# Attention: the prompt's scores, softmax and transpositions of a pair of heads queued ahead of the first half's units

## Chip, cores and metric

One core of a Trainium2 chip runs the whole program. The metric is the device time of one execution in microseconds (us). Three runs of the kernel before took 3154.69, 3155.14 and 3159.97 us; their median is 3155.14.

## What is computed

One inference step of a backbone with four layers. 512 latent tokens and 128 prompt (context) tokens of width 1024 run through them with the same weights. Each layer is a token mixer and a SwiGLU, both with adaLN modulation and a gated residual. The mixer of layer 0 is 2-D neighbourhood attention with a relative-position bias, of layer 1 banded sliding-window attention with a sink, of layer 2 multi-head latent attention, of layer 3 grouped-query attention; all have 16 heads. Cut to what matters for the change:

```python
def block_attention(q, k, v, sink=None):              # the prompt: its own keys only
    ...
    def one_block(qi):
        s = jnp.einsum('bqhgd,bkhd->bhgqk', qi, k).astype(jnp.float32) * scale
        (p,) = joint_softmax([s], sk)
        return jnp.einsum('bhgqk,bkhd->bqhgd', p.astype(v.dtype), v)

# in each layer
op = heads_out(block_attention(qp, kp_, vp_), na_w_o[r])                          # prompt
os_ = heads_out(na_latent_attention(qs, ks_, vs_, cache_na_k[:, r], ...), ...)    # latent tokens
xp = xp + mp[2] * op
xs = xs + ms[2] * os_
xp = xp + mp[5] * swiglu(...)
xs = xs + ms[5] * swiglu(...)
```

The 128 prompt tokens attend to themselves alone; the 512 latent tokens attend to a selection of latent keys and to 128 cached ones.

## The kernel before

Each fp32 product outside the scores is made of three matmuls of high and low parts (`whi`, `wlo`, `hh`, `hl`). A layer's attention runs in `Attn.units()` (line 955): 16 units u = 0 to 15, four groups g of four heads, two pairs of heads `pr` in each, two halves `hf` of the latent tokens (256 each) for every pair; u = 4g + 2pr + hf. `half_pair` (line 1140) is one unit. It calls `blocks`, which makes four blocks of 128 latent queries by one head: scores into a PSUM tile `S`, softmax (maximum on VectorE, exponentials on ScalarE, a reciprocal, scaling on GpSimd), transpositions of the probabilities through a PSUM tile `tp` (line 1055), and their copy to `pt` by ScalarE or VectorE in turn (lines 286 and 288). Then come the products with the values, `sm<-pt,v`, one run without gaps (`run_of`), and the output is put away.

Between the blocks `tick` (line 937) runs background jobs: the next group's projections, the preparation of its queries and keys, the output projection, the modulation of later stages. Their matmuls, mostly `sm<-whi,hh` and the like, fill TensorE while softmaxes run; they are called fillers below. Blocks are issued with a priority raised by `AHEAD` = 100. What stands in which place on each engine is set by the tile framework's scheduler, from the order of the program, the raised priorities and its own estimate of times; buffers of a tile are handed out in the order of the program. `S` has three buffers in layers 0 and 1 and two in layers 2 and 3, `tp` two, the prompt's `pp` and `ptp` one.

The prompt's part of a pair is `prompt` (line 1102), called through `prompt_group`. It takes one `S` tile, makes the 128 x 128 scores of two heads (4 matmuls, in layer 2 6), one maximum for both (`stp`, line 1116), two exponentials (`pp`, line 1122), a reciprocal (line 1128), two scalings (line 1130), two transpositions (`tp<-consts,pp`) and one copy (`ptp`). Its products with the values, `sm<-ptp,v`, stand in the run of the pair's second half, in both kernels.

In layer 0 a pair's keys are transposed (`tp<-consts,qs`), scaled into 64 partitions, and copied to the other 64 by a DMA from SP's queue, `k<-k` (`double`, line 1050). The same queue carries the biases (`bias<-in_nabias`, 576 KB each) and the modulation weights (`rawm<-in_wmod`, four of 512 KB in a burst).

Of the kernel before, what the change touches and what calls it, by code (L numbers as in the profile page):

```python
# [910 lines left out]
class Attn:  # L911
# [228 lines left out]
    def half_pair(self, g, pr, hf):  # L1140
        net = self.net
        u = 4 * g + 2 * pr + hf
        own = self.prompt_group(g, pr) if hf else None
        vals = self.blocks(g, pr, hf, u)
        with net.tc.high_priority(offset=AHEAD):
            o = net.ps()
            net.run_of(self.pv(o[:, :256], vals) + (self.pv(o[:, 256:384], own) if hf else []))
            self.put_o(self.o_tile(2 * g + pr), o[:, :256], hf)
            if hf:
                self.put(self.o_tile(2 * g + pr), slice(NL, T), o[:, 256:384])  # L1150
# [659 lines left out]
```

## Time and profile before

| | us |
|---|---|
| median of three runs | 3155.14 |
| profiled execution | 3159.6 |
| its span (first to last instruction) | 3157.8 |
| TensorE busy in it | 3021.5 (96%) |
| VectorE, ScalarE, GpSimd busy | 2112.1, 1518.0, 612.7 |
| four attention loops, first score to last product with values | 296, 204, 253, 203 |

The profile is of one execution. Times within it count from the start of the span. An engine's idle time ahead of an instruction is put down to whoever released the semaphore it waited for. The granted clock is TensorE's, as a share of full speed.

### The profile page before, as it was taken

How to read it: one execution, taken by the hardware profiler on the slowest of the kernel's cores; microseconds unless marked ns; L12 is line 12 of the kernel's file. 1: busy time of each engine (PE TensorE's matmuls, PEld its weight loads, DVE VectorE, ACT ScalarE, POOL GpSimd, SP SyncE). 2: the span in 40 equal slices, each digit the busy share in tenths (PEclk: the TensorE clock that was granted, in tenths of full speed). 3: DMA queues.
4: the chain of work that ended last, by engine and by line, in shares of the span. 5: the costliest groups of instructions: out<-in, count | busy, mean ns of one | idle time of the engine just before them, and what ended most of it. 6: DMA issues, size and time to landing. Idle time of an engine off the chain costs nothing. (4 is left out here: it accounts for less than half of the span.)

```text
span 3157.8 us, 57354 instructions
## 1 busy us (share of the span) xinstructions
PE 3021.5 (96%) x21997; PEld 2844.8 (90%) x21997; DVE 2112.1 (67%) x4442; ACT 1518.0 (48%) x3248; POOL 612.7 (19%) x691
## 2 busy tenths in 40 slices
PE   7998999999999999999988899999999999999999
PEld 6997889999988789999986678999998878999999
DVE  5555486666577768585767776857575765876765
ACT  4455453343346755242446675534243566543432
POOL 2453210000045430000025553000002553100000
PEclk9998999999999999999998999999999999999999
DMA  8347544232433333222214223432223211232322
GB/s 267 92 127 215 179 132 150 93 121 89 136 128 105 136 117 118 84 82 83 81 54 144 66 62 109 160 108 81 81 86 114 56 33 28 62 104 67 97 69 82
DMA packets 159025, 331.40 MB, mean 105 GB/s; under 512 B 18592, under 2 KB 40480, under 8 KB 158752
## 3 DMA queue, kind: packets, MB, share of 16 engines
q1 hardware_dynamic: 155584, 323.46, 33.0%
q10 hardware_dynamic: 3168, 4.28, 0.4%
q8 instruction: 173, 2.83, 0.4%
q14 instruction: 100, 0.82, 0.1%
HBM read 303.86 MB, written 4.28 MB: 98 GB/s over the span
## 5 line engine op out<-in xcount | busy, mean ns | idle before, releaser
L271 PE MATMUL big<-hl,whi 128*128 128x320 f32 x2688 | 814.9, 309 | 1.8 <-DVE hl L1045 1.8
L271 PE MATMUL big<-hh,whi 128*128 128x320 f32 x2688 | 811.1, 310 | 1.6 <-ACT whi L319 1.1
L271 PE MATMUL big<-hh,wlo 128*128 128x320 f32 x2688 | 808.5, 310 | 0.0
L319 ACT CAST whi<-raw 128x512 fp32r<-128x512 f32 (+2 forms) x644 | 387.4, 607 | 687.0 <-PE big L271 536.7
L320 POOL TENSOR_TENSOR wlo<-raw,whi 128x512 fp32r<-128x512 f32 (+2 forms) x148 | 206.9, 1413 | 1583.0 <-ACT whi L319 1550.4
L271 PEld LDWEIGHTS big<-hh,whi 128*128 128x128 f32 x2688 | 499.2, 188 | 10.3 <-issue 3.2
L271 PEld LDWEIGHTS big<-hl,whi 128*128 128x128 f32 x2688 | 501.4, 188 | 3.5 <-DVE hl L1045 2.8
L271 PEld LDWEIGHTS big<-hh,wlo 128*128 128x128 f32 x2688 | 499.4, 188 | 0.3
L320 DVE TENSOR_TENSOR wlo<-raw,whi 128x512 fp32r<-128x512 f32 (+1 forms) x496 | 330.6, 671 | 152.2 <-ACT whi L319 146.8
L319 ACT CAST whi<-sum 128x512 fp32r<-128x512 f32 x320 | 197.3, 620 | 278.6 <-PE big L271 240.7
L271 PE MATMUL big<-ah,wlo 128*128 128x320 f32 x1408 | 329.1, 309 | 0.0
L271 PE MATMUL big<-ah,whi 128*128 128x320 f32 x1408 | 329.0, 310 | 0.0
L271 PE MATMUL big<-al,whi 128*128 128x320 f32 x1408 | 328.5, 309 | 0.0
L1087 POOL TENSOR_SCALAR p<-p,st 128x640 f32<-128x640 f32 (+2 forms) x256 | 195.3, 768 | 300.2 <-DVE st L1086 177.3
L320 DVE TENSOR_TENSOR wlo<-sum,whi 128x512 fp32r<-128x512 f32 x320 | 218.5, 685 | 45.3 <-ACT whi L319 43.2
L609 DVE SCALAR_TENSOR_TENSOR x<-big,mod,x 128x128 f32<-128x128 f32 (+2 forms) x384 | 146.4, 433 | 152.7 <-PE big L271 151.7
L271 PEld LDWEIGHTS big<-ah,whi 128*128 128x128 f32 x1408 | 237.2, 188 | 1.3 <-issue 0.8
L271 PEld LDWEIGHTS big<-al,whi 128*128 128x128 f32 x1408 | 237.3, 188 | 0.3
L271 PEld LDWEIGHTS big<-ah,wlo 128*128 128x128 f32 x1408 | 237.3, 188 | 0.2
L271 PE MATMUL sm<-whi,hh 128*128 128x256 f32 (+1 forms) x770 | 224.9, 297 | 3.4 <-ACT qs L286 2.2
L271 PE MATMUL sm<-whi,hl 128*128 128x256 f32 (+1 forms) x770 | 223.6, 292 | 0.0
L271 PE MATMUL sm<-wlo,hh 128*128 128x256 f32 (+1 forms) x770 | 223.4, 292 | 0.1
(268 smaller groups left out, 5454.0 us busy)
## 6 DMA issues: line engine op xcount, KB each, us to landing
raw<-in_wall SPq DMA_DIRECT2D x676, 256.0 KB, 2.6
rawm<-in_wmod SPq DMA_DIRECT2D x176, 512.0 KB, 5.9
k<-k SPq DMA_DIRECT2D x38, 384.0 KB, 4.1
bias<-in_nabias SPq DMA_DIRECT2D x16, 576.0 KB, 7.2
raw<-in_wmod SPq DMA_DIRECT2D x32, 256.0 KB, 5.7
qpe<-pes SPq DMA_DIRECT2D x56, 80.0 KB, 2.1
raw<-in_wall SPq DMA_DIRECT2D x32, 128.0 KB, 2.1
out_y<-x ACTq DMA_DIRECT2D x8, 320.0 KB, 2.2
```

The costliest lines, as they stand in the source:

```text
L271: self.last_mm = self.nc.tensor.matmul(out, lhsT=lhsT, rhs=rhs, start=start, stop=stop, skip_group_check=True)
L319: self.nc.scalar.copy(hi, raw)
L320: eng.tensor_tensor(lo, raw, hi.bitcast(F32), ALU.subtract)
L609: self.last = self.nc.vector.scalar_tensor_tensor(xs, halves[b][:, p0:p1], self.mcol(L, i, d, c), xs, ALU.mult, ALU.add)
L1087: nc.gpsimd.tensor_scalar(p, p, rd, 1.0, ALU.mult, ALU.mult)
```

## The change

`prompt_group` is called in the first half's unit of a pair (hf = 0) rather than in the second's (hf = 1), and its result is kept in `self.own`. In both units the call stands ahead of `blocks`. The products with the prompt's values stay in the second half's run, as do their outputs.

```diff
--- before.py
+++ after.py
@@ -1140,7 +1140,9 @@
     def half_pair(self, g, pr, hf):
         net = self.net
         u = 4 * g + 2 * pr + hf
-        own = self.prompt_group(g, pr) if hf else None
+        if hf == 0:
+            self.own = self.prompt_group(g, pr)
+        own = self.own
         vals = self.blocks(g, pr, hf, u)
         with net.tc.high_priority(offset=AHEAD):
             o = net.ps()
```

The scheduler sets the order of the queues, so the diff doesn't show what moves. Three places follow, each as TensorE's queue before and now. First layer 0, between u5 and u6. Names carry the tile's number: `S_2715` is the first block of u6, `k_2382` the keys of its first head, `pp_2427` the prompt's exponentials of the pair before. Before:

```order
L271 MATMUL sm_2507<-whi_2503,hh_416 128x256
L271 MATMUL sm_2507<-wlo_2504,hh_416 128x256
L271 MATMUL sm_2507<-whi_2503,hl_417 128x256
L271 MATMUL S_2715<-k_2382,q_2282 128x256 [waits DMAHW3_49,DVE_49]
L271 MATMUL S_2715<-k_2382,q_2282 128x256
L271 MATMUL S_2715<-k_2382,q_2282 128x128 x2
L271 MATMUL sm_2561<-whi_2485,hh_188 128x256
L271 MATMUL sm_2561<-wlo_2486,hh_188 128x256
L1055 MATMUL tp_2433<-consts_78,pp_2427 128x128 [waits Pool_49]
```

Now, with `k_2400` and `k_2443` the keys of its two heads, `S_2673` the prompt's scores, and `S_2733` and `S_2789` the first two blocks:

```order
L271 MATMUL sm_2616<-whi_2503,hl_408 128x256
L271 MATMUL sm_2616<-whi_2503,hh_416 128x256
L271 MATMUL sm_2616<-wlo_2504,hh_416 128x256
L271 MATMUL sm_2616<-whi_2503,hl_417 128x256
L271 MATMUL S_2673<-k_2400,q_2300 128x128 [waits DMAHW6_49]
L271 MATMUL S_2733<-k_2400,q_2300 128x256 x2
L271 MATMUL S_2733<-k_2400,q_2300 128x128 x2
L271 MATMUL S_2789<-k_2443,q_2303 128x256 [waits DMAHW7_49]
L271 MATMUL S_2789<-k_2443,q_2303 128x256
L271 MATMUL S_2789<-k_2443,q_2303 128x128 x2
L271 MATMUL S_2673<-k_2400,q_2300 128x128
L271 MATMUL S_2673<-k_2443,q_2303 128x128 x2
```

The first use of the pair's keys is now the prompt's, at the end of a row of fillers, with the products of u5 (`sm_2658<-pt_2438`) 24 rows ahead of it; before, it was a block's, with those products 72 rows behind it. From the keys' transpositions to their first use there were 44 rows and are now 92.

TensorE, layer 0, between u11 and u12. `pt_3811` belongs to u11; `k_3752` (before) or `k_3770` (now) and `k_3812` are the keys of u12's heads. Before:

```order
L271 MATMUL sm_3942<-hh_3663,wlo_3939 128x320
L271 MATMUL sm_3972<-pt_3811,v_2120 64x256 [waits DVE_49,Activation_49]
L271 MATMUL sm_3972<-pt_3811,v_2120 64x256
L271 MATMUL sm_3972<-pt_3811,vs_2440 64x128 x4
L271 MATMUL sm_3972<-pt_3811,v_2120 64x128 x4
L271 MATMUL sm_3972<-ptp_3809,v_2120 64x128 x2
L271 MATMUL S_4005<-k_3752,q_3659 128x256 [waits DMAHW4_49]
L271 MATMUL S_4005<-k_3752,q_3659 128x256
L271 MATMUL S_4005<-k_3752,q_3659 128x128 x2
L271 MATMUL S_4060<-k_3812,q_3662 128x256 [waits DMAHW5_49]
```

Now, with `S_3989` the prompt's scores:

```order
L271 MATMUL sm_3884<-consts_78,modev_3882 128x8 x2
L271 MATMUL S_3989<-k_3770,q_3677 128x128 [waits DMAHW4_49]
L271 MATMUL S_4023<-k_3770,q_3677 128x256
L271 MATMUL S_4023<-k_3770,q_3677 128x256 [waits DVE_49]
L271 MATMUL S_4023<-k_3770,q_3677 128x128 x2
L1055 MATMUL tp_3967<-consts_78,p_3962 128x128 [waits Activation_49,Pool_49]
L1055 MATMUL tp_3967<-consts_78,p_3962 128x128 x2
L271 MATMUL sm_3905<-hh_3568,whi_3840 128x320 [waits DVE_49]
L271 MATMUL sm_3905<-hl_3569,whi_3840 128x320
L271 MATMUL sm_3905<-hh_3568,wlo_3841 128x320
L271 MATMUL S_4078<-k_3812,q_3680 128x256 [waits DMAHW5_49]
L271 MATMUL S_4078<-k_3812,q_3680 128x256
```

The first use of these keys moved ahead of the products of u11, which now stand 29 rows behind it; from the keys' transpositions it was 59 rows away and is 26. On SP's queue the copies of these keys stand behind a bias, four `rawm`, a bias in the order before, and behind four `rawm` and two biases now.

TensorE, layer 2, start of u4, where `S` has two buffers. `S_20507`, `S_20546` and `S_20585` are the first three blocks. Before:

```order
L271 MATMUL sm_20499<-whi_20376,hl_19261 128x384
L271 MATMUL S_20507<-k_20416,qn_20319 128x320 [waits DMAHW3_49]
L271 MATMUL S_20507<-k_20416,qn_20319 128x320 [waits DVE_49]
L271 MATMUL S_20507<-kpe_19051,qpe_20322 128x320 [waits DMAHW6_49,DMAHW5_49,DMAHW4_49]
L271 MATMUL S_20507<-k_20416,qn_20319 128x320 x2
L271 MATMUL S_20507<-kpe_19051,qpe_20322 128x320
L271 MATMUL S_20546<-k_20420,qn_20348 128x320 [waits DMAHW4_49]
L271 MATMUL S_20546<-k_20420,qn_20348 128x320 [waits DVE_49]
L271 MATMUL S_20546<-kpe_19051,qpe_20351 128x320 [waits DMAHW2_49,DMAHW7_49,DMAHW1_49,DMAHW0_49]
L271 MATMUL S_20546<-k_20420,qn_20348 128x320 x2
L271 MATMUL S_20546<-kpe_19051,qpe_20351 128x320
L271 MATMUL S_20585<-k_20416,qn_20319 128x320 [waits Activation_49]
```

Now, with `S_20498` the prompt's scores, `S_20527` and `S_20566` the first two blocks:

```order
L271 MATMUL S_20498<-k_20416,qn_20319 128x128 [waits DMAHW3_49]
L271 MATMUL S_20527<-k_20416,qn_20319 128x320
L271 MATMUL S_20527<-k_20416,qn_20319 128x320 [waits DVE_49]
L271 MATMUL S_20527<-kpe_19051,qpe_20322 128x320 [waits DMAHW6_49,DMAHW5_49,DMAHW4_49]
L271 MATMUL S_20527<-k_20416,qn_20319 128x320 x2
L271 MATMUL S_20527<-kpe_19051,qpe_20322 128x320
L271 MATMUL S_20498<-k_20416,qn_20319 128x128
L271 MATMUL S_20498<-kpe_19051,qpe_20322 128x128
L271 MATMUL S_20498<-k_20420,qn_20348 128x128 [waits DMAHW4_49]
L271 MATMUL S_20498<-k_20420,qn_20348 128x128 [waits DVE_49]
L271 MATMUL S_20498<-kpe_19051,qpe_20351 128x128 [waits DMAHW2_49,DMAHW7_49,DMAHW1_49,DMAHW0_49]
L271 MATMUL S_20566<-k_20420,qn_20348 128x320 [waits Activation_49]
```

The wait for ScalarE stood at the third block's first matmul; it now stands at the second block's, whose tile has to be free of the prompt's scores.

## Rows read from the trace of the kernel before

**Rows 1.** The page: busy time, share of the span and instructions of each engine.

```profile
PE 3021.5 (96%) x21997; PEld 2844.8 (90%) x21997; DVE 2112.1 (67%) x4442; ACT 1518.0 (48%) x3248; POOL 612.7 (19%) x691
```

**Rows 2.** Busy times by stretch, the sum of the four attention loops.

```profile
sum 956.00, PE 876.62 PEld 768.02 DVE 599.70 ACT 594.44 POOL 429.74; mean PE 219.16 PEld 192.00 DVE 149.92 ACT 148.61 POOL 107.43
```

**Rows 3.** Tile pp: ns min/median/max; who waited for it (us in all, times).

```profile
L1122 ACT ACTIVATE pp<-S,stp x64: 344/367/401, 110.3 to 2664.2; 128x128 f32<-128x128 f32 x64
...
  PE tp L1055: 1.3, 1
...
  PE S L271: 1.0, 3
```

**Rows 4.** TensorE's waits, layer 0 (us, times, longest); timeline at u2, u6, u14.

```profile
PE S L271 <- DMA k<-k: 7.2, 4, 2.3
...
137.24 0.67 PE L271 MATMUL S<-k,q 128*128 128x256 f32 x4 [1.48 <-DMA k<-k]
...
209.97 0.67 PE L271 MATMUL S<-k,q 128*128 128x256 f32 x4 [2.33 <-DMA k<-k]
...
347.62 1.12 PE L271 MATMUL S<-k,q 128*128 128x256 f32 x4 [1.75 <-DMA k<-k]
```

**Rows 5.** By stretch: busy PE, PEld, DVE, ACT, POOL; clock, DMA share, GB/s.

```profile
137.20:141.00 3.80, 3.76 (x32) 3.63 (x32) 1.15 (x5) 1.08 (x3) 0.63 (x2) 1.00 0.12 30
...
204.00:207.00 3.00, 3.00 (x29) 3.00 (x27) 1.72 (x6) 1.12 (x3) 1.12 (x2) 1.00 0.84 272
...
210.00:214.00 4.00, 4.00 (x23) 4.00 (x24) 0.73 (x3) 0.71 (x2) 0.58 (x1) 0.64 0.01 2
...
347.60:351.00 3.40, 3.38 (x15) 3.38 (x16) 0.77 (x3) 0.71 (x2) 0.00 (x0) 0.50 0.24 81
```

**Rows 6.** Timelines of TensorE and SP ahead of u12; the keys' copies there.

```profile
303.62 0.77 PE L1055 MATMUL tp<-consts,qs 128*128 128x128 f32 x5
...
317.65 1.60 PE L271 MATMUL S<-k,q 128*128 128x256 f32 x12
...
301.49 2.60 SPq L456 DMA_DIRECT2D rawm<-in_wmod  x4
306.09 0.33 SPq L1366 DMA_DIRECT2D bias<-in_nabias  x1
307.21 1.59 SPq L1052 DMA_DIRECT2D k<-k  x2
...
DMA to landing us min/median/max: 9.2/9.2/9.2
```

**Rows 7.** The same at u0.

```profile
77.42 0.71 PE L1055 MATMUL tp<-consts,qs 128*128 128x128 f32 x5
...
89.84 1.03 PE L271 MATMUL S<-k,q 128*128 128x256 f32 x8
...
81.65 2.02 SPq L1052 DMA_DIRECT2D k<-k  x2
...
DMA to landing us min/median/max: 3.7/4.3/4.9
```

**Rows 8.** Timeline of all engines, layer 2, start of u4.

```profile
1756.98 1.71 DVE L1076 TENSOR_REDUCE st<-S 128x1 f32<-128x640 f32 x2 [0.40 <-PE S L271]
...
1757.90 0.80 ACT L1077 ACTIVATE p<-S,st 128x640 f32<-128x640 f32 x1 [0.74 <-DVE st L1076]
...
1758.84 0.56 PE L271 MATMUL S<-k,qn 128*128 128x320 f32 x2 [1.01 <-ACT p L1077]
...
1765.04 0.41 DVE L1116 TENSOR_REDUCE stp<-S 128x2 f32<-128x256 f32 x1
...
1771.41 0.41 PE L1055 MATMUL tp<-consts,pp 128*128 128x128 f32 x2 [1.33 <-ACT pt L286]
```

**Rows 9.** Timeline of TensorE: end of layer 1's loop, start of layer 3's.

```profile
1134.15 0.98 PE L1055 MATMUL tp<-consts,p 128*128 128x128 f32 x7 [0.62 <-ACT pt L286]
...
2498.90 0.41 PE L1055 MATMUL tp<-consts,pp 128*128 128x128 f32 x2 [1.12 <-ACT pt L286]
```

## The prediction

> **What bounds the kernel now.** The page comes first: TensorE is busy for 96% of the span [rows 1], so a change that moves instructions and adds or removes none can only win or lose in the gaps of TensorE. The second view is the table of the four attention loops, from the first score to the last product with the values of each layer: in their 956.00 us TensorE is busy for 876.62 [rows 2]. Those 79.4 us of gaps, 2.5% of the span, are all that this change can reach. The third view is the prompt's own tile of exponentials: TensorE waited once, for 1.3 us, at the transpositions of it, and three times, 1.0 us in all, at a score tile that had to wait for it [rows 3]. So nearly nobody waits for the prompt's softmax where it stands now, and queueing it earlier saves no more than these 2.3 us directly. Everything else that can happen is a side effect: the prompt's scores are now the first use of a pair's keys, and its score tile is allotted ahead of four others. So I read next who ended TensorE's waits at the places where a pair or a group of heads starts [rows 4, 6 to 9].
>
> **Part by part.** Nothing is added and nothing removed: per pair of heads the same 4 score matmuls (6 in layer 2), one maximum, two exponentials, a reciprocal, two scalings, two transpositions and a copy, 32 pairs in four layers. No DMA is issued by the moved step itself, but the order of SP's queue around it changes in layer 0. The single buffers of the prompt's exponentials and of its transposed copy live one unit longer; the products with the values that free the copy stand ahead of the next pair's transpositions in both orders, so I cost that at nothing: the cover is the fillers between them, and the price without it is the 1.3 us of [rows 3] per pair. Now the gaps, one by one.
>
> *Layer 0, waits for the doubled keys.* Four pair starts (u2, u6, u10, u14) wait for the copy of the keys from one half of the partitions to the other, 7.2 us in all [rows 4]. In the order the stretch between the transpositions that make a pair's keys and their first use changes: at u2 from 48 rows of TensorE's queue to 94, at u6 from 44 to 92, at u10 from 39 to 37 (with longer matmuls in between), at u14 from 46 to 53. Fillers and the products of the unit before now stand where the bare wait stood. Those 46 and 48 extra rows at u2 and u6 are far more than the waits, so 1.48 and 2.33 us go; at u10 I take 0.3 off, at u14 0.9 (seven rows of 0.12 us or more, as the queue runs ahead of u0 [rows 7]). Two of the waits have a second price: after the 2.33 us of u6 the granted clock is 0.64 for 4 us, a mix of the two levels 1.2 and 2.4 GHz, after the 1.75 us of u14 it is 0.50, the lower level, for 3.4 us, while behind the 1.48 us of u2 it stays at 1.00 [rows 4, 5]. The first does 1.4 us less work, the second 1.7; both go, since what is left at u14, 0.85, is shorter than the wait of u2. Sum: 1.5 + 2.3 + 1.4 + 0.3 + 0.9 + 1.7 = **8.1 us gained**.
>
> *Layer 0, the same queue at u12.* Here it goes the other way. In the profile the keys' transpositions start at 303.62 and their first use at 317.65, 14.0 us and 59 rows of the queue later, with no wait for the copy: SP issued it at 307.21, behind four transfers of modulation weights and a bias, and it took 9.2 us to land, at about 316.4 [rows 6]. In the changed order the prompt's first matmul stands 26 rows behind the transpositions, ahead of 18 filler matmuls and of the products of u11. At the same pace 26 rows are 6.2 us, and the copy would land 12.8 us behind the transpositions' start: a wait of 6.6. SP's queue has both biases ahead of the copies now, one more than in this stretch before; if it delays them by its bytes, 0.58 MB at the 272 GB/s that the stretch before the wait of u6 moved [rows 5], that is 2.1 more, so 8.7 at most. At the least it is nothing, if the weight transfers ahead are issued earlier. I take the middle, 4.4, and with a wait of that length the clock's price of [rows 5], 1.5 between its two values: **5.9 us lost** (0 to 8.7 + 1.7 = 10.4).
>
> *Layer 0, the rest.* At u0 the copies are issued from 81.65 on and take 3.7 to 4.9 us to land, and the first score starts at 89.84, 12.4 us and 100 rows behind the transpositions [rows 7]. With 66 rows now, 8.2 us by the same pace, it would start at 85.6, when the first copy is landing and the second, issued up to 2 us later, is not: 1.0 lost (0 to 3.0). At u4 and u8 the second head's keys are needed some 40 rows earlier than before: 0.5 (0 to 1.0).
>
> *Layer 2, group starts (u4, u8, u12).* Score tiles have two buffers there. Before, two blocks' scores run back to back and the third waits 1.01 us for the first exponentials [rows 8]. Now the prompt's tile and the first block fill both buffers, no filler stands behind them, and the second block waits until the prompt's exponentials are done. From the end of the first block's scores that is a maximum of 0.86 us (1.71 for two), the block's exponentials of 0.80, then, with the prompt's maximum of 0.41 beside them, its own two of 0.37 [rows 3, 8], less the prompt's five matmuls that still run: about 2.2 us in place of 1.01. That is 1.2 more at three places, 3.6, and at one of them the wait of 1.33 ahead of the prompt's transpositions goes [rows 8]: **2.3 us lost**. The ends: 1.3 gained, if the ScalarE takes the prompt first, and 3 x (1.2 + 1.7) = 8.7 lost, if each bare wait also draws the clock down as at u14.
>
> *Layers 1 and 3.* The last unit of layer 1 has no prompt left in its way, and fillers come to stand between its transpositions, where 0.62 is lost at one now [rows 9]: 0.6 gained (0 to 0.6). In layer 3 the wait of 1.12 ahead of a pair's prompt transpositions goes [rows 9]: 1.1 gained (0 to 1.1).
>
> The sum: -8.1 + 5.9 + 1.0 + 0.5 + 2.3 - 0.6 - 1.1 = **-0.1 us**. The profiled execution took 3159.6, 4.5 above the median of 3155.14, and within the three runs' own spread (3154.69 to 3159.97); a difference of 0.1 carries over as it is. Forecast: 3155.14 - 0.1 = 3155.0, no change that a measurement can show.
>
> **The rivals.** *A, faster: the waits go and none comes.* The copy at u12 lands in time because the weights' transfers ahead of it go out earlier, and layer 2's wait is hidden. For it: at u2 and u6 the order leaves no doubt that the fillers cover the copies, and the 3.8 us of waits there are measured. Against it: at u12 the use comes 33 rows sooner. Time: -8.1 - 1.3 - 0.6 - 1.1 = -11.1, so 3144.
>
> *B, slower: the prompt's scores are a bare wait at the head of the queue.* At u12 of layer 0 and at the three group starts of layer 2 nothing stands between TensorE and a tile that isn't ready, and each such wait draws the clock down: 10.4 + 8.7 + 1.0 + 0.5 = 20.6 lost against 8.1 gained, and half of the 1.7 of layers 1 and 3: +11.7, so 3167. It decides from where the copy at u12 lands more than some 10 us behind the keys' transpositions and layer 2's waits are longer than the 1.48 us of u2, behind which the clock did not fall. For it: the 9.2 us of the copy in that very stretch against 3.7 in an empty one [rows 6, 7]. Against it: the scheduler put a wait of 14 us of work between keys and use there before, so it may have left the copy time in the new order too. The Trainium skill says in "DMA: Bandwidth & Descriptors", section "Queues, rings and completion order", that on each DMA engine the descriptors of an issuing engine's ring are consumed in ring order; by that the copy waits for all that SP issued before it, which speaks against this change at u12 and would give the 8.7 us end at u12, 3159.3 for the whole sum. The trace agrees as far as it goes: 9.2 us behind four weight transfers.
>
> *C: the change does little of what it says.* The framework's scheduler sets the queues by its own estimate of times, and about a fifth of TensorE's rows read differently after the change; what one wait gives back, the next takes, as those for ScalarE's copies of transposed probabilities in [rows 9]. Time: 3155, inside the forecast's own range.
>
> **How the numbers follow.** A measurement of this kernel can tell about 0.2%, 6.3 us, from no change. Forecast with C 0.45 (own range 3149 to 3161), A 0.30, B 0.25. The range reaches to A's time and to B's, 3144 to 3167; it leaves out what lies beyond both, some 2 in 10. Faster by over 0.2% 0.30, within it 0.45, slower 0.25.
>
> **What would show it.** In the trace of after: no wait for the keys' copy at u2 and u6 and no stretch of lower clock behind u6; one at u12 of 0 to 8.7 us (over 6 with a lowered clock speaks for B, none for A); in layer 2 at u4, u8 and u12 a wait of about 2.2 us of the second block's scores for the prompt's exponentials, where 1.01 stood; busy times of all engines as before. I am wrong altogether if the FFN stretches change, if TensorE's busy time changes by other than the clock, or if the gain comes from waits for the prompt's own results, which the trace prices at 2.3 us.

## The result, and the profile after

The changed kernel takes 3196.85 us (median of four runs, 3191.51 to 3203.36) against 3155.44 of the kernel before beside it. The ratio on record is 1.0121, with a 95% interval of 1.0108 to 1.0133: the change costs 38 us (34 to 42), and this figure is used below. (The two medians as they stand lie 41.4 us apart.) The forecast was 3155.0 in a range of 3144 to 3167; it was wrong.

The profiled execution of the changed kernel has a span of 3195.4 us, 37.6 more than before. First its page: busy time, share of the span and instructions of each engine.

```profile
PE 3036.8 (95%) x21997; PEld 2852.6 (89%) x21997; DVE 2118.5 (66%) x4442; ACT 1517.1 (47%) x3248; POOL 611.9 (19%) x691
```

As many matmuls as in [rows 1]; TensorE is busy 15.3 us longer with them, and idle 22.3 us longer. The view of cores gives the mean granted clock, here of the kernel before, of the changed one, and of a third kernel that comes below (softmax_early):

```profile
core 0: 3157.8 us, clock 0.983
...
core 0: 3195.4 us, clock 0.980
...
core 0: 3158.7 us, clock 0.985
```

A span times what its clock lacks to 1 is an estimate of what the clock takes: 53.7, 63.9 and 47.4 us, each good to some 1.6 us, as the clock is given in thousandths. So some 10 of the 37.6 us are clock. The four attention loops, from shortly ahead of the first score to the last product with values, as in [rows 2]:

```profile
sum 983.80, PE 890.51 PEld 774.75 DVE 602.13 ACT 594.39 POOL 440.22; mean PE 222.63 PEld 193.69 DVE 150.53 ACT 148.60 POOL 110.05
```

They are 27.8 us longer than in [rows 2], 93.3 us of them idle in place of 79.4. The other 10 us lie outside them, 5.6 of it as waits at the entries of the FFNs, of which more below. The list of TensorE's waits over the whole span (us in all, times, longest) shows where the idle time went. Kernel before:

```profile
PE tp L1055 <- ACT pt L286: 15.2, 19, 1.7
...
PE S L271 <- ACT p L1077: 10.1, 19, 1.6
PE S L271 <- DMA k<-k: 8.4, 7, 2.3
...
PE big L271 <- DVE hl L1045: 1.8, 4, 0.5
...
PE tp L1055 <- POOL pp L1130: 1.3, 1, 1.3
...
PE tp L1055 <- POOL p L1087: 0.6, 2, 0.4
```

Changed kernel:

```profile
PE tp L1055 <- ACT pt L286: 19.0, 21, 2.6
PE S L271 <- DMA k<-k: 15.5, 7, 6.7
...
PE S L271 <- ACT p L1077: 13.2, 19, 1.7
...
PE big L271 <- DVE hl L1045: 7.4, 4, 3.7
...
PE tp L1055 <- POOL p L1087: 4.2, 6, 1.5
...
PE tp L1055 <- POOL pp L1130: 3.1, 3, 1.9
```

Four groups grew most: transpositions (`tp`) that wait for GpSimd's scaling or for ScalarE's copies, by 9.2 us; the keys' copies, by 7.1; the FFN's first matmuls (`big`), by 5.6; scores that wait for exponentials, by 3.1. Which of them is the cause, and which follows from it, the list doesn't tell.

The places, in the order of time. In layer 0 the waits of [rows 4] at u2 and u6 are gone, as forecast. At u10 and u14 they are longer, and at u12 there is a new one. Timeline of SP and TensorE ahead of u10, then the three waits, then the copies there:

```profile
275.57 0.33 SPq L1368 DMA_DIRECT2D bias<-in_nabias  x1
276.00 2.32 SPq L309 DMA_DIRECT2D raw<-in_wall  x3
279.27 0.47 SPq L1052 DMA_DIRECT2D k<-k  x1
...
292.28 1.54 PE L271 MATMUL S<-k,q 128*128 128x128 f32 x6 [6.73 <-DMA k<-k]
...
319.38 0.79 PE L271 MATMUL S<-k,q 128*128 128x128 f32 x5 [2.15 <-DMA k<-k]
...
358.49 1.90 PE L271 MATMUL S<-k,q 128*128 128x128 f32 x10 [3.27 <-DMA k<-k]
...
DMA to landing us min/median/max: 12.3/12.6/13.0
```

The first copy at u10 goes out at 279.27 behind a bias and three weights, takes 13.0 us and ends the wait. That it takes long is not new. In the kernel before it went out 3.7 us sooner and took 10.8 us:

```profile
275.61 0.47 SPq L1052 DMA_DIRECT2D k<-k  x1
...
286.50 1.08 PE L271 MATMUL S<-k,q 128*128 128x256 f32 x4 [1.61 <-DMA k<-k]
...
DMA to landing us min/median/max: 10.8/12.6/14.4
```

The stretch behind the wait of 6.73 us, and the one behind u12's (busy times, then granted clock, DMA share and GB/s):

```profile
292.30:298.00 5.70, 4.81 (x21) 4.62 (x22) 2.27 (x9) 1.99 (x6) 0.62 (x2) 0.50 0.84 322
...
319.40:323.00 3.60, 3.60 (x27) 3.60 (x28) 1.43 (x6) 1.98 (x6) 0.58 (x1) 1.00 0.02 6
```

After 6.73 us of waiting the clock is at its lower level, 1.2 GHz, for the whole 5.7 us; after 2.15 us at u12 it is at 2.4 GHz. At the entries of the FFNs behind layers 0 and 1, TensorE's timeline has

```profile
393.52 0.61 PE L271 MATMUL big<-hh,whi 128*128 128x320 f32 x1 [3.65 <-DVE hl L1045]
...
1163.99 0.39 PE L271 MATMUL big<-hh,whi 128*128 128x320 f32 x1 [2.87 <-DVE hl L1045]
```

where the kernel before has

```profile
384.45 0.42 PE L271 MATMUL big<-hl,whi 128*128 128x320 f32 x1 [0.45 <-DVE hl L1045]
...
1142.27 0.41 PE L271 MATMUL big<-hl,whi 128*128 128x320 f32 x1 [0.44 <-DVE hl L1045]
```

And at the start of layer 3's loop, the timeline of all engines around the first transpositions:

```profile
2522.08 0.80 POOL L1087 TENSOR_SCALAR p<-p,st 128x640 f32<-128x640 f32 x1
...
2522.94 1.49 DVE L1004 TENSOR_TENSOR qs<-qs,ss 128x1280 f32<-128x1280 f32 x1
2524.34 0.16 DVE L1128 RECIPROCAL stp<-stp 128x2 f32<-128x2 f32 x1
...
2524.60 0.72 POOL L1130 TENSOR_SCALAR pp<-pp,stp 128x128 f32<-128x128 f32 x2 [1.72 <-DVE stp L1128]
...
2525.02 0.33 PE L1055 MATMUL tp<-consts,pp 128*128 128x128 f32 x1 [1.91 <-POOL pp L1130]
...
2525.19 0.60 PE L1055 MATMUL tp<-consts,p 128*128 128x128 f32 x4
```

The wait of 1.91 us is the line to remember. The first block's probabilities are scaled at 2522.88. Their transpositions start at 2525.19, 2.3 us later, and for 1.91 us of that TensorE is idle: the prompt's first transposition stands ahead of them in its queue. That one waits for a chain whose reciprocal got a later turn on VectorE, behind a product of 1.49 us; GpSimd stood idle for it for 1.72 us. Waits of this kind come at three places, 3.1 us in all (`POOL pp` in the list).

### The profile page after: what moved, and what is told of

It reads as the page before. It is cut to its first block, busy times and chain, and to the rows that moved or that the text cites. A ratio compares the mean times of both kernels' runs of the same rounds, so it can differ in the third digit from the quotient of the medians.

```text
span 3195.4 us, 57358 instructions
## 1 busy us (share of the span) xinstructions
PE 3036.8 (95%) x21997; PEld 2852.6 (89%) x21997; DVE 2118.5 (66%) x4442; ACT 1517.1 (47%) x3248; POOL 611.9 (19%) x691
## 4 chain that ended last, share of the span: by engine, by line
PE 86%; DVE 6%; DMA 4%; ACT 3%; issue 1%; POOL 0%; SPq 0%; ACTq 0%; DVEq 0%; POOLq 0%
PE big L271 56%; PE sm L271 17%; PE S L271 7%; PE tp L1055 4%; DMA k<-k 1%; DMA rawm<-in_wmod 1%; PE tp L271 1%; DVE st L1076 1%; ACT p L1077 1%; DMA raw<-in_wall 1%; DVE q L1045 0%; ACT pt L286 0%; ACT whi L319 0%; DVE x L609 0%; DVE qs L1004 0%
## 5 line engine op out<-in xcount | busy, mean ns | idle before, releaser
L320 POOL TENSOR_TENSOR wlo<-raw,whi 128x512 fp32r<-128x512 f32 (+2 forms) x148 | 199.5, 1360 | 1579.5 <-ACT whi L319 1555.2
```

The source lines that it names most:

```text
L320: eng.tensor_tensor(lo, raw, hi.bitcast(F32), ALU.subtract)
```

## The experiments

All runs are timed against the kernel before on the same chip; a figure in us is the ratio taken on 3155 us. In every diff `first` or the place of the call is all that differs, unless it is shown.

**The change in one layer at a time.**

```diff
-        own = self.prompt_group(g, pr) if hf else None
+        first = self.L == 0
+        if hf == (0 if first else 1):
+            self.own = self.prompt_group(g, pr)
+        own = self.own if hf else None
```

> The change in layer 0 alone. Read from the two traces, the whole change is 8.7 us behind at the last product with values of layer 0 and 12.7 us behind at the first matmul of the next layer's projections. Theory P (each place pays for itself): +12.7 us against the kernel before, most of it a wait of some 6.7 us for the keys' copy at u10 with a lowered clock behind it, and a wait of some 3.6 us at the start of the FFN. Rival H (the delays hand over: an order that is changed in one layer shifts the transfers of the next, and the layers do not add): under 5 us or over 20 us here.

Measured: 1.0038 (1.0027 to 1.0050), +12.0 us, as P expected. Its trace has two waits for the keys' copies at u10 (3.85 and 2.10 us), with the clock at 0.50 behind them, and 3.7 us at the start of the FFN.

> The change in layer 1 alone. Theory P: +13.5 us, as the delay grows from 12.7 to 26.2 us between the start of layer 1's projections and the start of layer 2's: 4 at the loop's start, 6.4 at u10, the rest at the start of the FFN. Rival H: layer 1's part came from the shift it inherited from layer 0, so within 4 us of the kernel before.

Measured: 1.0037 (1.0024 to 1.0049), +11.7 us.

> The change in layer 2 alone. Theory P: +6.0 us (the delay grows from 26.2 to 32.2 us over this layer), with waits of 2 us and more at the second block of u4, u8 and u12 for the prompt's exponentials. Rival H: within 2 us of the kernel before, or over 10 us.

Measured: 1.0008 (0.9996 to 1.0021), +2.5 us.

> The change in layer 3 alone. Theory P: +5.5 us, all of it ahead of the first products with values; the rest of the loop and the last FFN cost nothing. Rival H: within 2 us of the kernel before, or over 10 us. The four runs together: P wants a sum near 37.7 to 41 us.

Measured: 1.0014 (1.0001 to 1.0027), +4.4 us. The four make 30.6 us of 38, where P wanted 37.7 at the least; its four figures lie within the four intervals, and 38 is just within that of their sum. Layers 0 and 1 hold most. The rival H, that the delays hand over, is out for layers 0 and 1; for layers 2 and 3 the intervals are too wide to tell.

**The keys' copies on another queue**, in the changed kernel and in the kernel before:

```diff
-        self.nc.sync.dma_start(t[o].bitcast(F32), t[r].bitcast(F32))
+        self.nc.scalar.dma_start(t[o].bitcast(F32), t[r].bitcast(F32))
```

> The whole change, with the keys' copies (k<-k) issued from ScalarE's DMA queue, not from SP's behind weights and biases. Theory Q (a good third of the loss is the keys' copies, which the prompt's scores now need first and which stand in SP's ring behind megabytes of weights): the waits for k<-k of 13.7 us in layer 0 and the lowered clock behind them go, so about 10 to 14 us less than the changed kernel, +24 to +28 us on the kernel before. Rival R (the transfers share the same engines, so that the copy lands no sooner, or the waits return at another tile): within 4 us of the changed kernel, +34 to +42.

Measured: 1.0097 (1.0060 to 1.0133), +30.6 us, with an interval of 11 us to either side.

> The kernel before, with the same move of the keys' copies to ScalarE's queue: the control for the run beside it. Theory Q: its four waits for k<-k (7.2 us) and some 3 us of lowered clock go: 0 to 10 us faster. Rival R: within 3 us of the kernel before, or slower, since ScalarE now waits for the split of the keys ahead of each copy.

Measured: 0.9991 (0.9974 to 1.0007), no change that can be told. The change still costs 1.06% against its control, some 33 us (21 to 46 by the two intervals), though the waits for the copies shrank to 6.2 us in the changed kernel's trace (line of the list of waits):

```profile
PE S L271 <- DMA k<-k: 6.2, 5, 2.5
```

So most of the loss stays when these waits are cut to well under half. What share of it they hold is not shown, since the interval takes in the figures of both Q and R.

**How far forward the prompt's part stands.** Behind all four blocks of the first half, behind two, behind one; the change has it ahead of all four. For the first:

```diff
-        own = self.prompt_group(g, pr) if hf else None
         vals = self.blocks(g, pr, hf, u)
+        if hf == 0:
+            self.own = self.prompt_group(g, pr)
+        own = self.own
```

For the other two the call stands in `tick`, where t is u + 1/2 or u + 1/4.

> The prompt's part is called in the first half's unit as in the change, but behind that half's four blocks, so its score tile comes behind theirs and its scores are not the first use of the keys. Theory F (what costs is the place ahead of the first half's blocks: first use of the keys, and a score tile taken from the first blocks): most of the loss goes, +0 to +10 us on the kernel before. Rival G (what costs is that the prompt's work is gone from the second half, where it filled TensorE): +30 to +40 us as in the change.

Measured: 1.0001 (0.9985 to 1.0017). This place is nearly that of the kernel before, where the part stands ahead of the second half's blocks: counted in the two traces, the prompt's transpositions come at the same place among those of the blocks in all 32 pairs. So F is met, but against G the run says little.

> The prompt's part is called in the first half's unit behind the first two of its four blocks (both heads' keys have been used, two score tiles are ahead of the prompt's). Theory F (what costs is to be first: first use of the keys, first score tile of a unit): within 6 us of the kernel before. Rival D (every block that the prompt overtakes costs its share): half of the change's loss, +15 to +22 us.

Measured: 1.0044 (1.0029 to 1.0059), +13.9 us.

> The same behind the first block alone: the second head's keys and the second score tile are still first used by the prompt's part. Theory F: between +5 and +20 us, less than the change since half of the keys' waits and of the bare waits for a score tile are gone. Rival D: three quarters of the change's loss, +25 to +32 us.

Measured: 1.0085 (1.0064 to 1.0106), +26.8 us. With 0, 2, 3 and 4 blocks overtaken the loss is 0, 14, 27 and 38 us. It grows with each block, as D says, though for two blocks D wanted 15 at the least (interval 9 to 19). F, my theory that it costs to be first, falls: behind two blocks both heads' keys have been used and two score tiles are ahead, and it costs 14 us all the same.

**Without a layer's first pair, and without its last** (`first = u > 1`, `first = u < 14`):

> The change in all pairs of a layer but the first one, whose prompt part stays in the second half. In the changed kernel some 4 us are lost at the start of layer 1's loop and some 7 at layer 3's, nothing sure at layers 0 and 2. Theory P (each place pays for itself): 10 us less than the change, about +28 us. Rival (the starts only pass on what the scheduler has to place anyway): within 4 us of the change.

Measured: 1.0069 (1.0048 to 1.0091), +21.8 us. P's 28 lies within the interval, and its rival is out.

> The change in all pairs of a layer but the last one, whose prompt part stays in the second half. In the changed kernel the last units of layers 0 to 2 are 2.4, 3.7 and 2.4 us shorter, and the entries of the FFNs behind them 3.8, 4.0 and 2.8 us longer (a wait for the bank that the FFN's second accumulator takes over). Theory B (what the last unit gains is given back at the FFN's entry): within 4 us of the change, +34 to +41 us. Rival: the waits at the entries are a loss of their own, and go with the last pair: +26 to +31 us.

Measured: 1.0086 (1.0067 to 1.0105), +27.1 us. The first pairs of the four layers hold some 16 of 38 us, the last ones some 11, of eight pairs in a layer; each figure is good to some 7 us. Theory B, that the last unit's gain is given back, falls. But the rival is not shown by it, for the waits at the FFN's entry did not all go with the last pair; of 7.4 us the trace still has

```profile
PE big L271 <- DVE hl L1045: 4.3, 4, 2.9
```

With the part behind the first block alone they are 1.5 us, and the loss is 27 us all the same.

**The prompt's scores in another tile**:

```diff
-        s = net.ps("S")
-        s = (s[:, 0] if len(s.shape) == 3 else s)[:, :w]
+        s = net.ps("sm")[:, :w]
```

> The whole change, with the prompt's scores in a tile of the small PSUM pool rather than in one of the score pool (2 or 3 buffers), so that the first blocks keep their score tiles. Theory S (a good part of the loss is the score tile that the prompt takes from the first blocks: 3.0, 5.1 and 4.5 us at u4, u8 and u12 of layer 2, and the start of layers 1 and 3): 10 to 20 us less than the change, +18 to +28 us. Rival (it is the softmax chains that queue, not the tile, or the fillers now lack the tile): within 5 us of the change, or slower.

Measured: 1.0364 (1.0345 to 1.0383), +115 us. The small pool is the fillers' and the products' own; with a tile of it the change costs three times what it does without. Of the score tile this tells nothing.

**The prompt's part cut in two**: scores and softmax ahead of the first half's blocks as in the change, transpositions and copy ahead of the second half's as before. Against the changed kernel:

```diff
-        tp = net.ps("tp")[:, :w]
-        ...
-        return [[(values(e), pt[:, e * P:(e + 1) * P], 0)] for e in range(2)]
+        def rest():
+            tp = net.ps("tp")[:, :w]
+            ...
+            return [[(values(e), pt[:, e * P:(e + 1) * P], 0)] for e in range(2)]
+        return rest
...
-        own = self.own
+        own = self.own() if hf else None
```

> The change cut in two: scores and softmax of the prompt ahead of the first half's blocks, its transpositions and the copy ahead of the second half's, as before. Theory A (it costs to put the scores first: keys, score tile, maximum and exponentials ahead of the first blocks'): +30 to +40 us as in the change. Rival T (it is the transpositions, which wait for GpSimd in the middle of the first blocks and hold one of two transposition tiles): 0 to +12 us.

Measured: 1.0007 (0.9995 to 1.0019), +2.2 us. This settles which step costs. The prompt's scores and softmax stand where the change puts them (its first exponentials start at 88.8 us, at 89.6 in the changed kernel and at 110.3 before), and nearly nothing is lost. The list of waits has still the keys' copies and the exponentials, but the transpositions and the FFN's entry are down again:

```profile
PE S L271 <- ACT p L1077: 13.3, 19, 1.8
...
PE S L271 <- DMA k<-k: 12.0, 10, 3.1
PE tp L1055 <- ACT pt L286: 10.3, 16, 1.7
...
PE tp L1055 <- POOL p L1087: 3.9, 5, 2.1
...
PE big L271 <- DVE hl L1045: 0.9, 2, 0.4
```

The same place as above, the start of layer 3's loop:

```profile
2488.30 0.80 POOL L1087 TENSOR_SCALAR p<-p,st 128x640 f32<-128x640 f32 x1 [1.26 <-DVE st L1086]
...
2489.11 0.72 POOL L1130 TENSOR_SCALAR pp<-pp,stp 128x128 f32<-128x128 f32 x2
...
2489.55 0.71 PE L1055 MATMUL tp<-consts,p 128*128 128x128 f32 x5
...
2498.03 0.44 PE L1055 MATMUL tp<-consts,pp 128*128 128x128 f32 x2
```

The first block is scaled at 2489.10, and its transpositions start 0.45 us later; those of the prompt come when nobody waits for them.

**Inside the second half**, behind two of its blocks, and behind all four (the call in `tick`, and behind `self.blocks`, for hf = 1):

> The prompt's part stands behind two of the four blocks of the second half. Theory C (the loss is one of the halves: without the first unit of each layer the first halves went from 39.0 to 56.7 us of idle TensorE and from 11.9 to 24.0 us lost to the clock, the second halves only from 25.6 to 17.1 and 13.3 to 8.4; inside the second half the place costs and gains little): within 6 us of the kernel before. Rival D (the further forward, the dearer, some 9.5 us for each block): 14 to 24 us faster.

Measured: 1.0016 (1.0003 to 1.0030), +5.0 us.

> The prompt's part stands behind all four blocks of the second half, right ahead of the products with values that need it. Theory C: the chain of some 3 us (maximum, two exponentials, reciprocal, two scalings, transpositions, copy) is now waited for at the end of a pair where fillers don't cover it: +10 to +60 us. Rival D: 28 to 45 us faster.

Measured: 1.0030 (1.0013 to 1.0048), +9.5 us, just under what C expected. D falls here: further back is no faster. The growth with each block overtaken holds in first halves alone, and no place tried is cheaper than that in the kernel before.

**Middle pairs alone, keys on ScalarE's queue** (`first = 1 < u < 14`, with the queue's diff above):

> The change in units 2 to 13 of each layer alone, with the keys' copies on ScalarE's queue. Theory P (places add: of +38 us, 16 go with the first pair, 11 with the last, 5 with the queue, and the queue alone gives 3): +0 to +10 us on the kernel before. Rival (what is moved in the middle still pays its share of 6 pairs in 8, 28 us): +18 us or more.

Measured: 1.0050 (1.0033 to 1.0067), +15.8 us, between the two. Six pairs of eight keep less than six eighths of the loss, but more than what is left when the parts found before are taken off 38. The places don't add up neatly.

**No transposition tile for the prompt**: its transpositions go to the free half of its own score bank, in the changed kernel and in the kernel before.

```diff
         s = net.ps("S")
-        s = (s[:, 0] if len(s.shape) == 3 else s)[:, :w]
+        s = s[:, 0] if len(s.shape) == 3 else s
+        s, tp = s[:, :w], s[:, w:2 * w]
...
-        tp = net.ps("tp")[:, :w]
```

> The whole change, with the prompt's transpositions written into the free half of its own score bank, so that it takes none of the two transposition tiles; on TensorE's queue they stand where the change has them, within some ten rows. Theory Y (it costs that the prompt's transposition tile stands in the rotation ahead of the first blocks' tiles): most of the loss goes, 0 to +14 us on the kernel before. Rival Z (it costs that the transpositions stand in TensorE's queue in the middle of the first half's work): +28 us or more, as in the change.

Measured: 1.0075 (1.0055 to 1.0094), +23.7 us, between Y and Z.

> The kernel before, with the same tile for the prompt's transpositions: the control. Its score tile is held until the copy, some 2 us longer. Theory Y: within 8 us of the kernel before, since in second halves the tile costs little. Rival: a score tile held longer costs more than a transposition tile, +10 us or more; then the run beside it has to be read against this one.

Measured: 1.0022 (1.0008 to 1.0036), +6.9 us. Against this control the change costs 0.53%, some 17 us (9 to 24 by the two intervals), in place of 38. So about half of the loss goes with the transposition tile. The other half stays with transpositions that stand in TensorE's queue ahead of the first half's, or with a score tile held longer at that place; these two I have not told apart. The trace has more of both than the control's: scores wait 18.5 us for exponentials (12.4 there), and transpositions 11.3 us for GpSimd's scaling (4.6 there).

## Why the prediction was wrong

**The step that failed** is a term put at nothing: the prompt's transpositions and copy at their new place. They come up once, where the buffers "live one unit longer", and that is costed "at nothing", with the fillers between them and the next pair as cover. I asked how long the buffers live, and whether anyone waits for the prompt's results; [rows 3] says hardly, and that is still so: the wait for `pp` is 3.1 us in all. I didn't ask whom the transpositions keep waiting when they stand in TensorE's queue, and in a tile of which there are two, ahead of the first half's blocks. The runs put the loss there: 1.0121 with them early, 1.0007 with only scores and softmax early. Rival B had the sign and a bare wait at the head of the queue, but named the scores, and its 3167 is 30 us short.

**What stays open.** To stand ahead of four blocks doesn't cost by itself. Counted in the traces, the prompt's transpositions come ahead of all block transpositions of the second half in the kernel before and in softmax_early, and ahead of all of the first half's in the changed kernel, in each of the 32 pairs. Why they are cheap ahead of the second half and dear ahead of the first, and why mostly in layers 0 and 1, no run shows. Nor was it tried to keep them early and give the prompt's reciprocal and scaling an earlier turn.

**Where 37 us go when the direct wait is 3.1.** Against softmax_early, whose span is 36.7 us shorter, the changed kernel loses some 16.5 us to the clock, 8.7 in transpositions that wait for ScalarE's copies, 6.5 at the FFN's entries and 3.5 at the keys' copies; these make 35.2, and the other waits, longer and shorter, nearly cancel. The clock is the largest item. The others shrink when the transpositions are moved back; by which steps an early transposition reaches the FFN's entry or the keys' copies is not shown.

**Point by point.**
- u2 and u6: right, both waits are gone.
- u10 and u14: wrong in sign. I counted rows of TensorE's queue and not when the copies go out and land: forecast 1.3 and 0.85 us of waiting, measured 6.73 and 3.27. Of the 8.1 us gained, u10 and u14 were to give 2.9.
- u12: the mechanism right, the size too high: 4.4 and a lowered clock forecast, 2.15 without one measured. The copies took 6.4 to 6.6 us there, where 9.2 and more were reckoned.
- Layer 2's group starts: a wait of 2.2 us at the second block for the prompt's exponentials forecast, 1.39 at u4 and 1.35 at u8 measured, and not for these. ScalarE took the first block's exponentials first, and the second block's scores start as soon as these are done, at u4 while the prompt's run and at u8 ahead of them. So the tile that the second block waits for is the first block's, and not the prompt's, as I had read it out of the order of the queue. The scores' waits for exponentials, 13.2 us in all, are as long in softmax_early (13.3), which loses next to nothing: the term was real and of no weight.

```profile
1783.07 0.79 ACT L1077 ACTIVATE p<-S,st 128x640 f32<-128x640 f32 x1 [1.23 <-POOL sqh L995]
...
1783.85 0.36 ACT L1122 ACTIVATE pp<-S,stp 128x128 f32<-128x128 f32 x1
1784.01 0.56 PE L271 MATMUL S<-k,qn 128*128 128x320 f32 x2 [1.39 <-ACT p L1077]
```

- Layers 1 and 3: the waits of [rows 9] are gone as forecast, and 2.87 us at the FFN's entry and 1.91 at the start of the loop stand in their place. I had looked at what a place loses today, not at what takes its turn.
- "Those 79.4 us of gaps, 2.5% of the span, are all that this change can reach": wrong. The gaps bound what can be gained, not what can be lost: the FFN's entries lie outside the loops, and TensorE was busy 15.3 us longer with the same matmuls.
- The Trainium skill, "DMA: Bandwidth & Descriptors", section "Queues, rings and completion order", was weighed for u12. The end of 8.7 us that it was to speak for did not come: the copies there, behind four weights and two biases, took 6.4 to 6.6 us. At u10 the first took 13.0 us behind a bias and three weights; but the DMA engines' share is 1.05 from 283.0 to 292.3 us, and the run does not tell the place in the queue from the load. With the copies on another issuing engine's queue the change still cost 1.06% more than its control, so the rule, true or not, doesn't carry the result.

## What to carry to other kernels

When work is moved ahead in an engine's queue, price each of its instructions as something that others stand behind, at the time at which its inputs are really ready; a small softmax whose transpositions come up before its scaling is done can stop larger ones that are ready. Its early part (scores, exponentials) and its late part (transposition, copy) can be queued apart, and here only the early one was cheap to move. Cut the moved work in two as the first experiment: the longest wait in the new trace, 6.7 us for a copy, was a poor guide, since most of the loss stayed when the waits for the copies were cut from 15.5 to 6.2 us.

## What the runs showed of the hardware

By the estimate above the clock took 53.7 us of the kernel before, 63.9 of the changed one and 47.4 of softmax_early, for the same 21,997 matmuls. A wait is paid as idle time, and where the clock is lower behind it, as at u10 (0.50 for 5.7 us), a second time. Whether it falls does not follow from the wait's length alone: after 2.15 us of waiting at u12 it was granted in full for 3.6 us, after 1.75 at u14 before the change it was at the lower level for 3.4 us [rows 5].
